# The last gate tile made wide, with the first down-projection products between its own and its results joined by folds

## The chip, the cores and the metric

The kernel runs on one core of a Trainium2 chip. The metric is the device time of one execution in microseconds (us). PE is the matrix engine, DVE the vector engine, ACT the scalar engine, POOL the general engine (here it mostly issues DMAs that add into their target), SP the engine that issues the loads from HBM.

## The reference

One decoder layer over 512 tokens with 1024 features: attention and retention, a layer norm, then a feed-forward part, in float32. The change touches only the feed-forward part:

```python
gate, up = jnp.split(x @ w_gate_up, 2, axis=-1)
ffn = (jax.nn.silu(gate) * up) @ w_down
return layer_norm(DEEPNORM_ALPHA * x + ffn, ln_ffn_gain, ln_ffn_bias)
```

The hidden width is 2816, in 22 tiles of 128 columns.

## The kernel before

**Splits.** A float32 product is made of three passes on PE over rounded parts: high by high, high by low, low by high. `split` (L85) makes the high part with an ACT copy (L86, a CAST) and the low part with a DVE subtraction (L91) or, for some operands, with an ACT negation and an adding DMA issued by POOL (L88, L89).

**Gate tiles.** The 22 tiles `n` are computed one after another. Each takes seven products of a Strassen-like scheme, into three PSUM banks `ga`, `gb` and `gc`; the weights of the products are called A, B, C and D, and the tokens' parts `11`, `12`, `22`, `s1` to `s4`. A *narrow* product (`g_mm`, L999) is twelve matmuls of 256 columns: for each of four slices of the contraction high by high, low by high, high by low. A *wide* product (`g_run`, L986) puts the two parts of the tokens side by side: four matmuls of 512 columns with the high weights and four of 256 with the low weights. The wide result has two halves that still have to be added. That is done by a *fold* (L939): ACT copies the bank into a temporary, DVE adds another bank where needed, and POOL issues a DMA of 128 KB that adds the right half to the left one. Tiles 4 to 20 are wide (`wide`, L935), the first four and the last, 21, are narrow. In a wide tile the results `w1`, `w2`, `t2` and `t7` are each folded; `w_silu1` and `w_silu2` apply SiLU on ACT to the folded `w1` and `w2`, and `w_end` (L1050, L1051) multiplies them by the folded `t2` and `t7` on DVE, into `hu`.

**Order.** The kernel is scheduled by hand: what each engine does, it does in the order in which the code names it. `w_cycle(n)` runs a wide tile, with products of the tile before and the tile after between its own. `g_cycle(21)` runs the last one, with `prepare_down` between its steps, and `g_end(21)` (L1033 to L1035) finishes it on DVE without a fold.

**Down projection.** The left half of the output is accumulated in four banks `left` (`dl0` to `dl3`, one for 128 tokens each). `conv_w(0, m)` splits the weights of a pair of hidden tiles `m` into `dh(0, m)` and `dl(0, m)`, `conv_h(m)` the hidden values into `h0` and `h1`; `d_mm` makes six matmuls of 512 columns for a bank. Pairs 0, 1, then 2, 3 and 10 are done so. Pair 10 is tiles 20 and 21, so it needs `w_end(20)` and the end of tile 21. Then come 21 units `w_mm(i)` of twelve matmuls each (a Strassen-like scheme for the rest), whose weights come from loads `r1`, `r2a`, `r2b`, `r3a` and so on. These loads use three buffers `raw`: `r2a` takes the buffer of `r1_2`, `r2b` that of `r1_3`, `r3a` that of `r1_4`, each when the last reader of the old contents is done. `r1_2` and `r1_3` are read by an ACT copy, an ACT negation and an adding DMA of POOL (L89, `dlp<-r`). The weights of a unit have four buffers, and `t4_` (L1425) and `t2_` (L1421) combine loads on DVE.

An ACT instruction on `idle` (L1525) stands behind the last SiLU, so that the function table of the square root is loaded there.

Of the kernel before, what the change touches and what calls it, by code (L numbers as in the profile page):

```python
# [53 lines left out]
def hybrid_layer_kernel(ctx: ExitStack, tc: tile.TileContext, xT, x, pos, w0, wf, wt, wo,  # L54
# [18 lines left out]
    def tmp(name, dt=F32):  # L73
        return tp.tile([P, 512], dt, tag="t", name=name)
# [856 lines left out]
    def held(n):  # L931
        return n in (0, 1)


    def wide(n):  # L935
        return FIRST <= n < NF - 1

    def fold(t):
        nc.gpsimd.dma_start(t[:, :Q], t[:, Q:], accum_op=ALU.add)  # L939
# [41 lines left out]
    def g_run(n, acc, kind, i, q, first, low, last):  # L981
        w = gw[n, kind][low]
        full = gp[n][acc]
        for k in range(4):
            rhs = parts[q][:, k, 0] if low else parts[q][:, k].rearrange("p i c -> p (i c)")
            T.matmul(full[:, :Q] if low else full, lhsT=w[:, i * S + k * P:i * S + k * P + P], rhs=rhs,  # L986
                     start=first and not low and k == 0, stop=last and k == 3, skip_group_check=True)

    def g_mm(n, acc, kind, i, q, first, low_first=False):
        h, l = gw[n, kind]  # L990
        if wide(n):
            for low in (1, 0) if low_first else (0, 1):
                g_run(n, acc, kind, i, q, first, low, low != low_first)
            return
        steps = [(k, a, b) for k in range(4) for a, b in ((h, 0), (l, 0), (h, 1))]
        if n == 0:
            steps.sort(key=lambda x: x[2])
        for j, (k, a, b) in enumerate(steps):
            T.matmul(gp[n][acc], lhsT=a[:, i * S + k * P:i * S + k * P + P], rhs=parts[q][:, k, b],  # L999
                     start=first and j == 0, stop=j == 11, skip_group_check=True)  # L1000
# [30 lines left out]
    def g_end(n):  # L1031
        g = gp[n]
        V.tensor_tensor(g["t2"], g["t2"], g["c"], op=ALU.add)  # L1033
        V.tensor_tensor(g["h1"], g["h1"], g["t2"], op=ALU.mult)
        V.tensor_tensor(g["h2"], g["h2"], g["t7"], op=ALU.mult)  # L1035

    def w_take2(n):
        g = gp[n]
        V.tensor_tensor(g["t2"], g["t2"], g["c"], op=ALU.add)  # L1039
        fold(g["t2"])  # L1040
# [4 lines left out]
    def w_silu2(n):  # L1045
        A.activation(gp[n]["h2"], gp[n]["w2"][:, :Q], AF.Silu)

    def w_end(n):
        g = gp[n]
        V.tensor_tensor(g["h1"], g["h1"], g["t2"][:, :Q], op=ALU.mult)  # L1050
        V.tensor_tensor(g["h2"], g["h2"], g["t7"][:, :Q], op=ALU.mult)  # L1051

    def w_copy2(n):
        g = gp[n]
        g["w2"] = tmp(f"w2_{n}")
        A.copy(g["w2"], g["a"])
        fold(g["w2"])

    def w_cycle(n):
        first, last = n == FIRST, n + 1 == NF - 1  # L1060
        p, nxt, g = n - 1, n + 1, gp[n]
        if first:
            g_mm(n, "a", "A", 0, "s2", False, True)
            g_end(p)
        else:
            g_run(p, "a", "C", 1, "22", False, 0, True)
            w_copy2(p)
            g_sum2(nxt)
            g_conv(n, "C")
            g_run(p, "c", "D", 0, "s4", False, 0, False)  # L1070
            g_run(n, "a", "A", 0, "s2", False, 0, False)
        g["c"] = psu(f"gc{n}")
        g_run(n, "c", "A", 1, "s1", True, 0, False)
        g_open(nxt)
        if not last:
            g_run(nxt, "a", "B", 0, "11", True, 0, False)
        if not first:
            g_run(n, "a", "A", 0, "s2", False, 1, True)
            g_run(p, "c", "D", 0, "s4", False, 1, True)
        g_run(n, "c", "A", 1, "s1", True, 1, True)  # L1080
        if last:
            g_mm(nxt, "a", "B", 0, "11", True)
        else:
            g_run(nxt, "a", "B", 0, "11", True, 1, True)
        if not first:
            if wide(n - 2):
                w_end(n - 2)
            g_conv(n, "D")
            g_load(n + 3)
            w_take2(p)  # L1090
        g["t2"] = tmp(f"t2_{n}")
        A.copy(g["t2"], g["a"])  # L1092
        g_conv(nxt, "A")
        g_mm(n, "a", "C", 0, "s3", False, True)
        g_t1(nxt)
        w_silu1(n)
        g["t7"] = tmp(f"t7_{n}")
        A.copy(g["t7"], g["a"])
        if last:
            g_mm(nxt, "b", "B", 1, "12", True)  # L1100
        else:
            for low in range(2):
                g_run(nxt, "b", "B", 1, "12", True, low, low == 1)
        g_sum3(nxt)
        V.tensor_tensor(g["t7"], g["t7"], g["c"], op=ALU.add)
        fold(g["t7"])
        g_run(n, "a", "C", 1, "22", False, 1, False)
        g_sum01(n + 2)
        g_u1(nxt)
        if wide(p):  # L1110
            w_silu2(p)
        g_conv(n + 2, "B")
        if last:
            g_run(n, "a", "C", 1, "22", False, 0, True)
            g_mm(n, "c", "D", 0, "s4", False)
            g_conv(nxt, "C")
            w_copy2(n)
            g_conv(nxt, "D")
            w_end(p)

    def g_cycle(n, between=None):
        nxt = n + 1 if FIRST <= n + 1 < NF else None
        g_mm(n, "a", "A", 0, "s2", False)
        if n and wide(n - 1):
            w_take2(n - 1)
        elif n and not held(n - 1):
            g_end(n - 1)
        if between:
            next(between)
        gp[n]["c"] = psu(f"gc{n}")[:, :Q]  # L1130
        g_mm(n, "c", "A", 1, "s1", True)
        t = tmp(f"gt{n}")
        gp[n]["t2"], gp[n]["t7"] = t[:, :Q], t[:, Q:]
        A.copy(gp[n]["t2"], gp[n]["a"])
        if n == 1:
            for m in range(FIRST):
                g_silu1(m)
        if n not in (1, 2, 3):
            g_conv(n + 1, "A")
        if nxt:  # L1140
            g_open(nxt)
            g_mm(nxt, "a", "B", 0, "11", True)
        g_mm(n, "a", "C", 0, "s3", False)
        if nxt:
            g_t1(nxt)
            g_mm(nxt, "b", "B", 1, "12", True)
        if held(n - 1):
            g_mm(n - 1, "c", "D", 0, "s4", False)
        if n == 0:
            g_mm(3, "b", "B", 1, "12", True)  # L1150
        c = gp[n]["c"]
        if n == NF - 1:
            c = tmp("gc")[:, :Q]
            A.copy(c, gp[n]["c"])
            g_mm(n, "c", "D", 0, "s4", False)
        A.copy(gp[n]["t7"], gp[n]["a"])
        if n == 0:
            for b in (2, 3):
                combine("s4", b)
                hi("s4", b)  # L1160
            g_sum(1, V, slice(2, 4))
        if n == 1:
            g_conv(2, "A")
            g_sum(2, V, slice(2, 4))
        V.tensor_tensor(gp[n]["t7"], gp[n]["t7"], c, op=ALU.add)
        if n in (2, 3):
            g_conv(n + 1, "A")
        if between:
            next(between)
        if n == 2:  # L1170
            g_end(n - 1)
        if n + 2 >= FIRST:
            g_conv(n + 2, "B")
        if n == 0:
            g_add1(3)
        g_mm(n, "a", "C", 1, "22", False)
        if nxt:
            g_u1(nxt)
        if n > 2:
            g_sum01(n + 2)  # L1180
            g_sum2(n + 2)
        g_conv(n + 1, "C")
        if n == 1:
            g_end(0)
        if n in (1, 2):
            g_sum(n + 2)
        if n == 0:
            for b in (2, 3):
                lo("s4", b)
            g_sum(2, V, slice(0, 2))  # L1190
        if n < NF - 1 and not held(n):
            g_mm(n, "c", "D", 0, "s4", False)
        if wide(n - 1):
            w_silu2(n - 1)
        A.activation(gp[n]["h2"], gp[n]["a"], AF.Silu)
        g_conv(n + 1, "D", V if n else None)
        g_load(n + 4)
# [300 lines left out]
        V.scalar_tensor_tensor(y[b][:, cs], in0=y[b][:, cs], scalar=r[:, 0:1], in1=gf[:, 1, cs], op0=ALU.mult, op1=ALU.add)  # L1498
        dma(out[b * P:(b + 1) * P, cs], y[b][:, cs])

    def prepare_down():
        conv_w(0, 0)
        conv_h(0)
        yield
        conv_w(0, 1)
        conv_h(1)
        yield

    for n in range(FIRST):
        g_cycle(n)  # L1510
# [2 lines left out]
    d_load(0, 0)  # L1513
    w_cycle(NF - 2)
    d_load(0, 1)
    g_cycle(NF - 1, prepare_down())
    g_end(NF - 1)

    def r1_load(j):
        r1[j] = raw_load(f"r1_{j}", [(2 * q, wd[2 * j + q, :, 0]) for q in range(2)])  # L1520
# [1 line left out]
    def r4_load(j):  # L1522
        r4[j] = raw_load(f"r4_{j}", [(2 * q, wd[2 * j + q, :, :, S:]) for q in range(2)])

    A.activation(idle, idle, AF.Sqrt)  # L1525
    left = [psu(f"dl{b}") for b in range(NB)]
    r1_load(2)
    d10 = [tmp(f"d10_{i}") for i in range(2)]
    for i in range(2):
# [1 line left out]
    r1_load(3)  # L1531
    conv_w(0, 2)
    conv_h(2)
    for b in range(3):
        for i in range(2):
            d_mm(left[b], 0, i, b, i == 0, False)
    conv_w(0, 3)
    r1_load(4)
    conv_h(3)
    for i in range(2):  # L1540
        d_mm(left[3], 0, i, 3, i == 0, False)
    for j in UNITS:
        s1_(j)
    for j in UNITS:
        aprep(1, j, blk(j, 0, 0), None)
    w_end(NF - 2)
    conv_h(10)
    t1_(2)
    conv_w(0, 10)
# [232 lines left out]
```

## Time and profile before

| | |
|---|---|
| median of 3 runs | 609.21 us (609.1 to 609.33) |
| the profiled execution | 609.27 us |
| its span, first to last instruction | 607.4 us |
| PE busy | 599.9 us (99%) |
| DVE busy | 517.3 us (85%) |
| ACT busy | 359.9 us (59%) |
| POOL busy | 187.8 us (31%) |
| stage of the last gate tile (its first to its last product) | 473.71 to 488.03 us |

A row of the timeline gives the start and the length of one or several merged instructions, engine, line, operation, target and sources, shape and count; a bracket names the idle time of the engine ahead of it and what ended it. `q1` is the queue of SP's loads, `q0` that of POOL's DMAs. A row of DMA issues gives count, size of each and the time from issue to landing.

### The profile page before, as it was taken

How to read it: one execution, taken by the hardware profiler on the slowest of the kernel's cores; microseconds unless marked ns; L12 is line 12 of the kernel's file. 1: busy time of each engine (PE TensorE's matmuls, PEld its weight loads, DVE VectorE, ACT ScalarE, POOL GpSimd, SP SyncE). 2: the span in 40 equal slices, each digit the busy share in tenths (PEclk: the TensorE clock that was granted, in tenths of full speed). 3: DMA queues.
4: the chain of work that ended last, by engine and by line, in shares of the span. 5: the costliest groups of instructions: out<-in, count | busy, mean ns of one | idle time of the engine just before them, and what ended most of it. 6: DMA issues, size and time to landing. Idle time of an engine off the chain costs nothing.

```text
span 607.4 us, 9356 instructions
## 1 busy us (share of the span) xinstructions
PE 599.9 (99%) x3280; PEld 522.2 (86%) x3280; DVE 517.3 (85%) x945; ACT 359.9 (59%) x633; POOL 187.8 (31%) x208
## 2 busy tenths in 40 slices
PE   8999999999999999999999999999999999999996
PEld 7988888888888888889998888888888988888885
DVE  6879976897997898989999898988889888988756
ACT  5454444434662766777657776776777685675300
POOL 0038732332363000342013444435344321241010
PEclk9999999999999999999999999999999999999999
DMA  8887864698984765596348888888887889699602
GB/s 280 251 249 195 219 208 123 151 225 225 204 174 108 278 227 202 126 249 129 87 154 202 165 208 164 209 188 186 205 173 191 183 224 204 158 249 228 249 35 105
DMA packets 50575, 115.25 MB, mean 190 GB/s; under 512 B 9136, under 2 KB 24816, under 8 KB 45024
## 3 DMA queue, kind: packets, MB, share of 16 engines
q1 hardware_dynamic: 25808, 77.68, 38.8%
q0 software_dynamic: 24416, 36.64, 34.8%
q8 instruction: 26, 0.43, 0.3%
q10 hardware_dynamic: 304, 0.33, 0.2%
q14 instruction: 21, 0.17, 0.1%
HBM read 74.52 MB, written 2.10 MB: 126 GB/s over the span
## 4 chain that ended last, share of the span: by engine, by line
PE 96%; DVE 2%; ACT 1%; DMA 1%; SPq 0%; issue 0%
PE ga L986 16%; PE gc L986 8%; PE pf L94 5%; PE pf L95 5%; PE pf L96 5%; PE ga L999 5%; PE gb L986 4%; PE pt L95 4%; PE pt L94 4%; PE pt L96 3%; PE acc L218 2%; PE dl L96 2%; PE dl L94 2%; PE dl L95 2%; PE gc L999 2%; PE mx L96 2%
## 5 line engine op out<-in xcount | busy, mean ns | idle before, releaser
L86 ACT CAST wh<-raw 128x1024 fp32r<-128x1024 f32 x44 | 46.0, 1048 | 30.6 <-issue 11.4
L939 POOL DMA_DIRECT2D t<-t x34 | 29.2, 858 | 75.2 <-DVE t L1039 43.7
L94 PE MATMUL pf<-xh,wh 128*128 128x512 f32 x128 | 50.0, 391 | 0.0
L95 PE MATMUL pf<-xl,wh 128*128 128x512 f32 x128 | 49.9, 390 | 0.0
L96 PE MATMUL pf<-xh,wl 128*128 128x512 f32 x128 | 49.9, 389 | 0.0
L91 DVE TENSOR_TENSOR wl<-raw,wh 128x1024 fp32r<-128x1024 f32 x26 | 33.1, 1281 | 12.0 <-ACT wh L86 12.0
L939 POOL DMA_DIRECT2D w<-w x34 | 29.5, 1002 | 41.9 <-DVE w L1025 39.7
L94 PE MATMUL pt<-wh,xh 128*128 128x512 f32 (+1 forms) x96 | 38.5, 402 | 0.0
L95 PE MATMUL pt<-wl,xh 128*128 128x512 f32 (+1 forms) x96 | 37.0, 386 | 0.0
L96 PE MATMUL pt<-wh,xl 128*128 128x512 f32 (+1 forms) x96 | 36.7, 382 | 0.0
L481 POOL TENSOR_TENSOR rs<-ve,half 128x1 f32<-128x1 f32 (+1 forms) x10 | 10.5, 1051 | 77.6 <-DVE ve L480 77.5
L89 POOL DMA_DIRECT2D wl<-raw x18 | 16.6, 922 | 45.2 <-ACT wl L88 44.3
L96 PEld LDWEIGHTS pf<-xh,wl 128*128 128x128 f32 x128 | 24.0, 188 | 5.2
L95 PEld LDWEIGHTS pf<-xl,wh 128*128 128x128 f32 x128 | 24.1, 188 | 4.6
L94 PEld LDWEIGHTS pf<-xh,wh 128*128 128x128 f32 x128 | 24.0, 188 | 4.6
L443 DVE MAX8 m<-score 128x8 f32<-128x256 f32 (+2 forms) x48 | 26.8, 557 | 1.0
L444 DVE MATCH_REPLACE8 score<-m,score 128x256 f32<-128x256 f32 (+2 forms) x48 | 26.0, 542 | 0.0
L954 POOL DMA_DIRECT2D graw<-graw x17 | 24.6, 1448 | 1.3 <-issue 0.9
L426 ACT ACTIVATE lg<-lg 128x256 f32<-128x256 f32 (+2 forms) x24 | 10.8, 474 | 22.7 <-PE lg L425 20.7
L1092 ACT COPY t<-ga 128x512 f32<-128x512 f32 x17 | 10.0, 588 | 22.9 <-PE ga L986 22.9
L89 POOL DMA_DIRECT2D slot<-hu x9 | 10.8, 1272 | 33.5 <-ACT slot L88 28.7
L96 PEld LDWEIGHTS pt<-wh,xl 128*128 128x128 f32 x96 | 18.0, 188 | 3.3
(1220 smaller groups left out, 2012.8 us busy)
## 6 DMA issues: line engine op xcount, KB each, us to landing
graw<-in_wgu_dram SPq DMA_DIRECT2D x22, 1024.0 KB, 5.1
wl<-raw POOLq DMA_DIRECT2D x18, 512.0 KB, 5.2
raw<-in_wo_dram SPq DMA_DIRECT2D x8, 1024.0 KB, 4.8
raw<-in_wf_dram SPq DMA_DIRECT2D x7, 1024.0 KB, 6.4
raw<-in_wt_dram SPq DMA_DIRECT2D x6, 1024.0 KB, 5.5
r<-in_wd_dram SPq DMA_DIRECT2D x12, 512.0 KB, 6.3
w<-w POOLq DMA_DIRECT2D x34, 128.0 KB, 2.8
graw<-graw POOLq DMA_DIRECT2D x17, 256.0 KB, 4.1
```

The source lines that it names most:

```text
L86: A.copy(hi, src)
L89: nc.gpsimd.dma_start(lo.bitcast(F32), src, accum_op=ALU.add)
L91: eng_lo.tensor_tensor(lo, src, hi.bitcast(F32), op=ALU.subtract)
L94: T.matmul(acc, lhsT=lh, rhs=rh, start=first, stop=False, **kw)
L95: T.matmul(acc, lhsT=lh, rhs=rl, start=False, stop=False, **kw)
L96: T.matmul(acc, lhsT=ll, rhs=rh, start=False, stop=last, **kw)
L443: V.max(m8, a)
L444: V.match_replace(out=a, in_to_replace=m8, in_values=a, imm_value=TAKEN)
L939: nc.gpsimd.dma_start(t[:, :Q], t[:, Q:], accum_op=ALU.add)
L954: nc.gpsimd.dma_start(u[:, :S], u[:, S:], accum_op=ALU.add)
L986: T.matmul(full[:, :Q] if low else full, lhsT=w[:, i * S + k * P:i * S + k * P + P], rhs=rhs, start=first and not low and k == 0, stop=las ...
L999: T.matmul(gp[n][acc], lhsT=a[:, i * S + k * P:i * S + k * P + P], rhs=parts[q][:, k, b], start=first and j == 0, stop=j == 11, skip_group ...
```

## The change

Tile 21 becomes wide. `w_cycle(20)` loses its special ending, `g_cycle` its branch for the last tile, and a new `w_last(21)` takes the place of `g_cycle(21)`, `prepare_down` and `g_end(21)`. It puts the products of tile 21 between the last ones of tile 20, and the first products of the down projection (pair 0, banks 0, 1 and 2) between the last ones of tile 21. The results `w1`, `w2`, `t2` and `t7` of tile 21 are folded. `w_silu2(21)`, ahead of the table load, stands behind the split of pair 2; `w_end(20)` and `w_end(21)` stand ahead of the split of pair 10.

```diff
     def wide(n):
-        return FIRST <= n < NF - 1
+        return n >= FIRST
...
     def w_cycle(n):
...
-        if last:
-            g_mm(nxt, "a", "B", 0, "11", True)
-        else:
-            g_run(nxt, "a", "B", 0, "11", True, 1, True)
+        g_run(nxt, "a", "B", 0, "11", True, 1, True)
...
-        if last:
-            g_run(n, "a", "C", 1, "22", False, 0, True)
-            g_mm(n, "c", "D", 0, "s4", False)
-            g_conv(nxt, "C")
-            w_copy2(n)
-            g_conv(nxt, "D")
-            w_end(p)
...
+    def left_mm(m, b):
+        d_mm(left[b], 0, m, b, m == 0, False)
+
+    def w_last(n):
+        p, g = n - 1, gp[n]
+        g_run(n, "a", "A", 0, "s2", False, 1, False)
+        g_run(p, "a", "C", 1, "22", False, 0, True)
+        w_copy2(p)
+        g_run(n, "a", "A", 0, "s2", False, 0, True)
+        g_conv(n, "C")
+        g_run(p, "c", "D", 0, "s4", False, 0, False)
+        g["c"] = psu(f"gc{n}")
+        g_run(n, "c", "A", 1, "s1", True, 0, False)
+        g_run(p, "c", "D", 0, "s4", False, 1, True)
+        g_run(n, "c", "A", 1, "s1", True, 1, True)
+        g["t2"] = tmp(f"t2_{n}")
+        A.copy(g["t2"], g["a"])
+        w_end(p - 1)
+        g_conv(n, "D")
+        w_take2(p)
+        g_mm(n, "a", "C", 0, "s3", False, True)
         conv_w(0, 1)
+        g["t7"] = tmp(f"t7_{n}")
+        A.copy(g["t7"], g["a"])
+        V.tensor_tensor(g["t7"], g["t7"], g["c"], op=ALU.add)
+        fold(g["t7"])
+        left_open()
+        left_mm(0, 0)
         conv_h(1)
-        yield
+        w_silu2(p)
+        w_silu1(n)
+        g_mm(n, "a", "C", 1, "22", False)
+        w_copy2(n)
+        left_open()
+        left_mm(0, 1)
+        g_mm(n, "c", "D", 0, "s4", False)
+        w_take2(n)
+        for b in (2, 3):
+            left_open()
+        left_mm(0, 2)
...
     d_load(0, 1)
-    g_cycle(NF - 1, prepare_down())
-    g_end(NF - 1)
+    conv_w(0, 0)
+    conv_h(0)
+    w_last(NF - 1)
...
-    A.activation(idle, idle, AF.Sqrt)
-    left = [psu(f"dl{b}") for b in range(NB)]
...
     conv_w(0, 2)
     conv_h(2)
+    w_silu2(NF - 1)
+    A.activation(idle, idle, AF.Sqrt)
     for b in range(3):
-        for i in range(2):
-            d_mm(left[b], 0, i, b, i == 0, False)
+        left_mm(1, b)
     conv_w(0, 3)
...
-    w_end(NF - 2)
+    for n in (NF - 2, NF - 1):
+        w_end(n)
     conv_h(10)
```

On PE, at the end of tile 20's products, before (`ga21` is bank `ga` of tile 21, `gh21A` the high part of its weights A):

```order
L986 MATMUL gc20_5006<-parts4_2890,gh20D_5039 128x512 x4
L986 MATMUL gc20_5006<-parts4_2890,gl20D_5040 128x256 x4
L999 MATMUL ga21_5011<-parts2_2692,gh21A_5047 128x256
L999 MATMUL ga21_5011<-parts2_2692,gl21A_5048 128x256
L999 MATMUL ga21_5011<-parts2_2692,gh21A_5047 128x256 x2
```

And now, from the last run of tile 20 to the first matmuls of the down projection:

```order
L986 MATMUL gc20_5006<-parts4_2890,gl20D_5036 128x256 x4
L986 MATMUL gc21_5116<-parts1_2756,gl21A_5044 128x256 x4
L986 MATMUL ga21_5011<-parts3_2695,gl21C_5107 128x256 x4
L986 MATMUL ga21_5011<-parts3_2695,gh21C_5106 128x512 x4
L94 MATMUL dl0_5155<-dh(0, 0)_5083,h0_0_5087 128x512
L95 MATMUL dl0_5155<-dl(0, 0)_5084,h0_0_5087 128x512
L96 MATMUL dl0_5155<-dh(0, 0)_5083,h1_0_5088 128x512
```

Tile 21's product with A now runs ahead of tile 20's end, and six matmuls of bank `dl0` stand between the two products with C, where the one with D stood.

On ACT, around the last SiLU (L1046 is `w_silu2`, into `hu5`; L1525 before and L1545 now is the instruction on `idle`, with its table load), before:

```order
L1046 ACTIVATE hu5_4900<-w2_20_5105 128x256
L1195 ACTIVATE hu5_4900<-ga21_5011 128x256
L1525 ACT_TABLE_LOAD
L1525 ACTIVATE idle_312<-idle_312 128x4
L86 CAST dh(0, 2)_5220<-draw0_1_5114 128x1024
L86 CAST h0_1_5224<-hu1_3175 128x1024
L86 CAST dh(0, 3)_5264<-draw0_1_5114 128x1024
```

And now (L1056 is the copy of the bank in `w_copy2`):

```order
L1056 COPY w2_21_5174<-ga21_5011 128x512
L86 CAST dh(0, 2)_5212<-draw0_1_5080 128x1024
L86 CAST h0_1_5216<-hu1_3175 128x1024
L1046 ACTIVATE hu5_4900<-w2_21_5174 128x256
L1545 ACT_TABLE_LOAD
L1545 ACTIVATE idle_312<-idle_312 128x4
L86 CAST dh(0, 3)_5240<-draw0_1_5080 128x1024
```

The last SiLU read a bank of PE; it now reads `w2_21`, which POOL's fold completes, and all that ACT does for the pairs 3 and 10 and for `r1` stands behind it.

On POOL, the end of the folds, before:

```order
L939 DMA w2_20_5105<-w2_20_5105 128x256
L939 DMA t2_20_5045<-t2_20_5045 128x256
L89 DMA slot0_5291<-hu2_3589 128x2x256
L89 DMA slot0_5291<-hu3_4026 128x2x256
L89 DMA slot1_5298<-hu4_4463 128x2x256
```

And now:

```order
L939 DMA w2_20_5099<-w2_20_5099 128x256
L939 DMA t2_20_5041<-t2_20_5041 128x256
L939 DMA t7_21_5151<-t7_21_5151 128x256
L939 DMA w2_21_5174<-w2_21_5174 128x256
L939 DMA t2_21_5129<-t2_21_5129 128x256
```

Three folds of tile 21 follow that of `t2_20`; the fourth, of `w1_21`, stands ahead of `w2_20`.

More of the change, by code (lines that the diff above doesn't have):

```diff
@@ L1059, in w_cycle @@
     def w_cycle(n):
-        first, last = n == FIRST, n + 1 == NF - 1
+        first = n == FIRST
         p, nxt, g = n - 1, n + 1, gp[n]
@@ L1074, in w_cycle @@
         g_open(nxt)
-        if not last:
-            g_run(nxt, "a", "B", 0, "11", True, 0, False)
+        g_run(nxt, "a", "B", 0, "11", True, 0, False)
         if not first:
@@ L1098, in w_cycle @@
         A.copy(g["t7"], g["a"])
-        if last:
[L1100 to L1103, printed above, removed]
+        g_mm(nxt, "b", "B", 1, "12", True)
         g_sum3(nxt)
@@ L1112, in w_cycle, with g_cycle @@
         g_conv(n + 2, "B")
-        if last:
-            g_run(n, "a", "C", 1, "22", False, 0, True)
-            g_mm(n, "c", "D", 0, "s4", False)
-            g_conv(nxt, "C")
-            w_copy2(n)
-            g_conv(nxt, "D")
-            w_end(p)
-    def g_cycle(n, between=None):
+    def g_cycle(n):
         nxt = n + 1 if FIRST <= n + 1 < NF else None
         g_mm(n, "a", "A", 0, "s2", False)
-        if n and wide(n - 1):
-            w_take2(n - 1)
-        elif n and not held(n - 1):
+        if n and not held(n - 1):
             g_end(n - 1)
-        if between:
-            next(between)
         gp[n]["c"] = psu(f"gc{n}")[:, :Q]
@@ L1151, in g_cycle @@
         c = gp[n]["c"]
[L1152 to L1155, printed above, removed]
         A.copy(gp[n]["t7"], gp[n]["a"])
@@ L1167, in g_cycle @@
             g_conv(n + 1, "A")
-        if between:
-            next(between)
         if n == 2:
@@ L1190, in g_cycle @@
             g_sum(2, V, slice(0, 2))
-        if n < NF - 1 and not held(n):
+        if not held(n):
             g_mm(n, "c", "D", 0, "s4", False)
-        if wide(n - 1):
-            w_silu2(n - 1)
         A.activation(gp[n]["h2"], gp[n]["a"], AF.Silu)
@@ L1499, in scale_bias, with left_open @@
         dma(out[b * P:(b + 1) * P, cs], y[b][:, cs])
-    def prepare_down():
-        conv_w(0, 0)
-        conv_h(0)
-        yield
-        conv_w(0, 1)
-        conv_h(1)
-        yield
+    left = []
+    def left_open():
+        left.append(psu(f"dl{len(left)}"))
+    def left_mm(m, b):
[18 more added lines that the diff above has]
+        g_mm(n, "a", "C", 0, "s3", False, True)
+        conv_w(0, 1)
+        g["t7"] = tmp(f"t7_{n}")
[4 more added lines that the diff above has]
+        left_mm(0, 0)
+        conv_h(1)
+        w_silu2(p)
[9 more added lines that the diff above has]
+        left_mm(0, 2)
     for n in range(FIRST):
@@ L1539, in hybrid_layer_kernel @@
     conv_h(3)
-    for i in range(2):
-        d_mm(left[3], 0, i, 3, i == 0, False)
+    for m in range(2):
+        left_mm(m, 3)
     for j in UNITS:
```

## The prediction

> **What bounds the kernel now.** I first read the waits of PE, from 460 us to the end. There is one, in the last microseconds:
>
> ```profile
> PE fin L1712 <- ACT diag L1711: 1.3, 1, 1.3
> ```
>
> From the last gate tiles on, matmuls follow each other without a gap, so only two things can move the end here: fewer or shorter matmuls, or a new wait of PE. The timeline of PE gives the pitch of both shapes, and the chain that ended last the period of a wide tile:
>
> ```profile
> 471.37 1.07 PE L986 MATMUL gc<-parts,gh20A 128*128 128x512 f32 x4
> 472.28 0.64 PE L986 MATMUL ga<-parts,gl20A 128*128 128x256 f32 x4
> 472.75 0.64 PE L986 MATMUL gc<-parts,gl19D 128*128 128x256 f32 x4
> ...
> 473.00 0.59 ACT L1092 COPY t<-ga 128x512 f32<-128x512 f32 x1 [0.59 <-PE ga L986]
> ...
> 473.71 0.28 PE L999 MATMUL ga<-part,gh21B 128*128 128x256 f32 x1
> ...
> 475.15 0.64 PE L986 MATMUL ga<-parts,gl20C 128*128 128x256 f32 x4
> ...
> 476.56 0.28 PE L999 MATMUL gb<-part,gh21B 128*128 128x256 f32 x1
> ...
> 477.98 0.64 PE L986 MATMUL ga<-part,gl20C 128*128 128x256 f32 x4
> ...
> 480.77 0.28 PE L999 MATMUL ga<-parts,gh21A 128*128 128x256 f32 x1
> ...
> 488.03 0.40 PE L94 MATMUL dl<-dh(0, 0)_5131,h 128*128 128x512 f32 x1
> 488.26 0.40 PE L95 MATMUL dl<-dl(0, 0)_5132,h 128*128 128x512 f32 x1
> ...
> 455.28 1.89 PE ga L986 x12
> 465.03 1.89 PE ga L986 x12
> ```
>
> **The gain.** The seven narrow products of tile 21 take 1.44 (473.71 to 475.15), 1.42 and 7.26 us (five, 480.77 to 488.03): 10.12. Seven wide ones take the period of a wide tile, 465.03 - 455.28 = 9.75. So PE gains **0.37 us**. The columns are the same, 3072 a product; only four short matmuls fewer are issued. The down projection's matmuls are the same ones in another order, at no price.
>
> **Inside the tile.** From 472.28 on I lay the runs in their new order: 0.91 us for four of 512, 0.48 for four of 256, 0.23 for a matmul of the down projection (488.03 to 488.26). ACT copies a bank in 0.59, from 0.08 behind the end of the run (473.00, after 472.28 + 0.64). Each accumulation into `ga21` that follows a copy of the bank must wait for ACT. The tightest place is the copy for `t7_21`: the run ahead of it ends at 485.0, the copy at 485.7, and the six matmuls of `dl0` (1.36 us) hold PE until 486.2. They hide it by 0.5; without them it would cost about 0.7. The others have as much or more, so I put this part at 0, and at 0.7 for its worse end.
>
> **The new wait.** The last product with C ends near 487.8 in the new order. ACT copies `w2_21` until 488.45; POOL answers such a copy 0.29 us later (481.17 after 480.30 + 0.58), so the fold is issued at 488.75. Now `w_silu2(21)` waits for its landing, and behind it on ACT stand the table load, pair 3, six operations on `slot`, pair 10, and the copies of `r1`. Before, that SiLU read PSUM, 0.30 us behind PE.
>
> ```profile
> 480.30 0.58 ACT L1056 COPY w<-ga 128x512 f32<-128x512 f32 x1
> 481.17 0.86 POOL L939 DMA_DIRECT2D w<-w  x1 [1.95 <-ACT w L1056]
> 488.23 0.38 ACT L1195 ACTIVATE hu<-ga 128x256 f32<-128x256 f32 x1 [0.30 <-PE ga L999]
> 490.04 1.03 ACT L86 CAST dh(0, 2)_5220<-draw 128x1024 fp32r<-128x1024 f32 x1
> ```
>
> How long does a fold take? The profile's page says 2.8 us for those of `w` and 4.7 for those of `t`, and single windows show why they differ:
>
> ```profile
> w<-w POOLq DMA_DIRECT2D x34, 128.0 KB, 2.8
> t<-t POOLq DMA_DIRECT2D x34, 128.0 KB, 4.7
> ...
> 483.68 0.86 POOL L939 DMA_DIRECT2D t<-t  x1 [1.66 <-DVE t L1039]
> ...
> q1 hardware_dynamic: 268, 0.95, 97.4%
> t<-t POOLq DMA_DIRECT2D x1, 128.0 KB, 8.0
> ...
> q1 hardware_dynamic: 281, 0.52, 74.8%
> q0 software_dynamic: 129, 0.12, 38.5%
> ```
>
> The two `q1` rows are of 484 to 488 and of 488 to 490 us. The fold issued at 483.68 moved nothing for four microseconds, in which the loads filled the engines; its 0.12 MB went through after 488, and it landed after 8.0 us. So a fold waits for the loads issued ahead of it. Those loads are these:
>
> ```profile
> 481.43 0.69 DVE L91 TENSOR_TENSOR gl21D<-graw,gh21D 128x512 fp32r<-128x512 f32 x1 [0.23 <-ACT gh21D L86]
> 482.15 0.83 SPq L80 DMA_DIRECT2D r<-in_wd_dram  x2
> 483.08 0.96 SPq L80 DMA_DIRECT2D d<-in_wd_dram  x2
> 486.70 1.23 DVE L91 TENSOR_TENSOR dl(0, 1)_5183<-draw,dh(0, 1)_5182 128x1024 fp32r<-128x1024 f32 x1 [0.52 <-ACT dh(0, 1)_5182 L86]
> 487.96 7.47 SPq L80 DMA_DIRECT2D r<-in_wd_dram  x4
> ```
>
> `r1_2` was issued as `gl21D` freed its buffer, `r1_3` as `dl(0, 1)` did. In the new order `gl21D` must wait for its buffer until the low half of tile 20's D has run, at 483.15, and ends at 483.94: `r1_2` goes at 484.0, with `d10` behind it. `dl(0, 1)` moves ahead, to 485.7, so `r1_3` goes at 485.9. That is 2.6 MB back to back, all issued before the fold of `w2_21`, with two other folds ahead of it on its queue. I take the nearest row, 8.0 us: **landing at 496.75**. At the 0.95 MB that 484 to 488 moved, the loads alone need 11 us from 485.5, to 496.5; with three folds of 0.77 us (38.5% of two) behind them, the upper end is 10 us, 498.8. The lower end is 2.8 us, 491.55.
>
> The Trainium skill ("DMA: Bandwidth & Descriptors", section "Queues, rings and completion order") says that each DMA engine takes turns between the queues for which it has work, packet by packet. By that a fold would not wait for the loads, and the sum would be that of rival A below, 608.9 to 610.8. In the windows above it did wait, so I go by them.
>
> **What follows from it.** ACT's next weights came 1.81 us behind the last SiLU (488.23 to 490.04). So `dh(0, 3)` starts at 498.7 and the high part of pair 3 ends at 500.7; DVE takes 1.14 for its low part, 1.8 for three sums, 1.36 for four halves of `w_end`, and the split of pair 10 starts at 505.2 where it was at 498.30: **6.9 us late**. From there on ACT's order is dense except for 0.77 us ahead of the second `dhp<-r`, so that copy is 6.1 late.
>
> ```profile
> 498.30 1.05 ACT L86 CAST h<-hu 128x1024 fp32r<-128x1024 f32 x1 [1.24 <-DVE hu L1051]
> 504.62 1.05 ACT L86 CAST dhp<-r 128x1024 fp32r<-128x1024 f32 x1 [0.77 <-ACT slot L86]
> ...
> 506.93 1.19 POOL L89 DMA_DIRECT2D dlp<-r  x1 [3.14 <-DVE tw L1411]
> 513.55 2.88 SPq L80 DMA_DIRECT2D r2b<-in_wd_dram  x4
> 516.53 1.79 SPq L80 DMA_DIRECT2D r3a<-in_wd_dram  x4
> ...
> 523.14 2.68 DVE L1425 TENSOR_TENSOR tw<-r3a,r2a 128x512 f32<-128x512 f32 x4 [0.26 <-DMA r3a<-in_wd_dram]
> ...
> 529.34 2.35 DVE L91 TENSOR_TENSOR dlp<-r2a,dhp 128x1024 fp32r<-128x1024 f32 x2
> ...
> 531.80 0.39 PE L95 MATMUL dx<-dlp,slot 128*128 128x512 f32 x1
> ```
>
> The chain to PE: the adding DMA of 506.93 follows that copy; `r2b` waits for its landing (513.55), as it takes the buffer of `r1_3`; `r3a` stands behind `r2b` on SP; DVE already waits for `r3a` now (0.26 at 523.14), and behind that DVE is dense until the low weights of unit 6, the first of the two in the row at 529.34 (ready at 530.56, half of 2.35 later). PE reads them at 531.80. So the slack is 1.24 us, and 0.37 less when PE comes earlier: 0.87. With the chain 6.1 late, PE stalls **5.2 us** there. (Unit 1, five times twelve matmuls earlier, reads what the adding DMA makes; 513.4 + 6.1 is 1.7 us after its 517.8, a part of the same 5.2.) Behind unit 6, PE needs new weights every 2.7 us and DVE makes them in 1.2; I expect no more.
>
> **Sum.** 609.27 (this execution; the median of the three is 0.06 lower) - 0.37 + 5.2 = **614.1 us**. In general: a landing of L us puts the chain L - 1.9 late and stalls PE by L - 2.8. Its ends are 608.9 (L = 2.8, no stall) and 616.1 (L = 10).
>
> **Rivals.**
>
> *A. The fold does not queue behind the loads.* Then it lands after 2.8 us, or up to the 4.7 of the `t` row when it shares the engines with them. At 2.8, the stall is 0 and the time 608.9; at 4.7 it is 1.9, and 610.8. The point from which it decides is L = 3.2, where stall and gain cancel. For it: the folds of `w` took 2.8, 34 of them. Against: none of these was issued behind a load, and the next row shows what one does (window 495 to 499, in which three folds of `slot` were issued, the first at 495.26, behind the loads of `r1_4`):
>
> ```profile
> q1 hardware_dynamic: 132, 0.51, 75.7%
> slot<-hu POOLq DMA_DIRECT2D x3, 256.0 KB, 7.7
> ```
>
> No byte of these moved while the loads ran. Its likeliest time is 609.3, not slower than before. The rule of the Trainium skill that stands above ("DMA: Bandwidth & Descriptors") is this rival's.
>
> *B. The wait is there, but the slack is larger:* `r3a` lands as early as before, because with other loads shifted the queue is emptier. Then the stall is unit 1's alone, 1.7, and the time 610.6; with the adding DMA quicker by its queueing it would be 609 to 610. Against: `r3a` cannot be issued before `r2b`, nor that before the adding DMA has read its buffer.
>
> *C. The loads hold the fold longer* (L of 10 to 12): 616.1 to 618.1.
>
> *D. PE waits inside the tile as well,* by the 0.7 above once or twice: that is hidden in the sum if the later stall comes, as that is set by ACT's chain, and alone it gives 609.6 to 610.3.
>
> **How the numbers follow.** Main case (L of 5.5 to 10, 611.6 to 616.1): 0.58. A: 0.20, B and D with little stall: 0.15, C: 0.05; a shortening of PE's work by over 1.2 us that I do not see: 0.02. What differs by less than 0.2% (1.2 us, 608.0 to 610.4) can't be told from no change. All of A up to L = 4.3 and two thirds of B and D lie there: 0.28. Faster: 0.02. Slower: 0.70. The range runs from A's lower end, 608.8, to 616.3, which leaves out C and little else.
>
> **What would show it.** In the changed kernel's trace: wide products of tile 21 without a gap (the matmuls from the first with `gh21B` to the last of tile 21 and the eighteen of the down projection between them); `r1_3` issued near 486; the fold of `w2_21` landing near 497 and ACT's `hu<-w` waiting for a DMA for some 6 us ahead of the table load; `h<-hu` of pair 10 near 505; `r3a` near 522.5; PE waiting for DVE's `dlp` at unit 6, with a first wait at unit 1. A landing before 492 and no wait of PE would prove rival A. A wait of PE between 472 and 490 would prove D.

## The result, and the profile after

| | before | after |
|---|---|---|
| median | 609.27 us (6 runs, 608.92 to 609.56) | 612.66 us (6 runs, 612.22 to 613.13) |
| ratio | | 1.0052, 95% interval 1.0042 to 1.0063 |
| span of the profiled execution | 607.4 us | 610.9 us |

The changed kernel is 3.4 us slower; 614.1 was forecast. The waits of PE from 460 us on, where there was one before:

```profile
PE fin L1724 <- ACT diag L1723: 1.3, 1, 1.3
PE dx L95 <- DVE dlp L91: 1.1, 1, 1.1
PE dx L95 <- DMA dlp<-r: 1.1, 1, 1.1
PE dy L95 <- DVE dlp L91: 0.3, 1, 0.3
```

No wait lies inside the tile; the three new ones are at units 1 (`dx`, for an adding DMA), 5 (`dy`) and 6 (`dx`, for low weights of DVE). The profiled executions aren't aligned in this stage: the run with `gh20A`, which the change doesn't touch, starts at 471.69 and not 471.37, so **0.32 us** is to be taken off a time of after before it is compared. The timeline of PE, with that run, the first matmul of pair 2, and the places where the pitch (the time from one start to the next, 0.227 us here) breaks:

```profile
471.69 1.07 PE L986 MATMUL gc<-parts,gh20A 128*128 128x512 f32 x4
...
498.88 0.39 PE L94 MATMUL dl<-dh(0, 2)_5212,h 128*128 128x512 f32 x1
...
509.76 0.39 PE L94 MATMUL dl<-dh(0, 10)_5289,h 128*128 128x512 f32 x1
510.10 0.50 PE L95 MATMUL dl<-dl(0, 10)_5290,h 128*128 128x512 f32 x1
510.44 0.39 PE L96 MATMUL dl<-dh(0, 10)_5289,h 128*128 128x512 f32 x1
...
518.18 0.39 PE L94 MATMUL dx<-dhp,slot 128*128 128x512 f32 x1
519.64 0.50 PE L95 MATMUL dx<-dlp,slot 128*128 128x512 f32 x1 [1.07 <-DMA dlp<-r]
519.98 0.39 PE L96 MATMUL dx<-dhp,slot 128*128 128x512 f32 x1
...
531.10 0.50 PE L95 MATMUL dy<-dlp,slot 128*128 128x512 f32 x1 [0.29 <-DVE dlp L91]
...
535.24 0.50 PE L95 MATMUL dx<-dlp,slot 128*128 128x512 f32 x1 [1.12 <-DVE dlp L91]
```

*The gain is there.* From the run with `gh20A` to pair 2, PE needs 498.88 - 471.69 = 27.19 us; before, the same stretch took 498.94 - 471.37 = 27.57. That is 0.38 less, where 0.37 was forecast.

*The loss.* A place loses what two starts are apart beyond 0.227, in the pitch at the wait and the one behind it: 0.23 at pair 10, 1.35 at unit 1, 0.56 at unit 5, 1.40 at unit 6, in all **3.5 us**. With the gain, 3.5 - 0.4 = 3.1. From the run with `gh20A` to the first matmul of `fin`, near the end, PE needs 132.15 us where it needed 128.86, 3.3 more and near the 3.4 between the medians; the missing tenth or two is in the next pitches behind each wait, of 0.23 to 0.24 us.

The chain behind it, in the timelines of ACT, DVE, POOL and SP:

```profile
488.13 0.59 ACT L1056 COPY w<-ga 128x512 f32<-128x512 f32 x1 [0.59 <-PE ga L986]
489.01 0.86 POOL L939 DMA_DIRECT2D w<-w  x1 [1.16 <-ACT w L1056]
497.50 0.42 ACT L1046 ACTIVATE hu<-w 128x256 f32<-128x256 f32 x1 [6.88 <-DMA w<-w]
499.33 1.03 ACT L86 CAST dh(0, 3)_5240<-draw 128x1024 fp32r<-128x1024 f32 x1
505.93 1.05 ACT L86 CAST h<-hu 128x1024 fp32r<-128x1024 f32 x1 [1.48 <-DVE hu L1051]
507.02 1.23 DVE L91 TENSOR_TENSOR h<-hu,h 128x1024 fp32r<-128x1024 f32 x1 [1.12 <-ACT h L86]
511.39 1.05 ACT L86 CAST dhp<-r 128x1024 fp32r<-128x1024 f32 x1
513.70 1.19 POOL L89 DMA_DIRECT2D dlp<-r  x1 [2.27 <-DVE slot L91]
519.72 1.75 SPq L80 DMA_DIRECT2D r2b<-in_wd_dram  x4
521.57 2.54 SPq L80 DMA_DIRECT2D r3a<-in_wd_dram  x4
527.96 2.49 DVE L1398 TENSOR_TENSOR tw<-r3a,r2a 128x512 f32<-128x512 f32 x4
533.97 2.35 DVE L91 TENSOR_TENSOR dlp<-r2a,dhp 128x1024 fp32r<-128x1024 f32 x2
...
w<-w POOLq DMA_DIRECT2D x1, 128.0 KB, 8.4
```

The bracket at 497.50 is the new wait: ACT stands for 6.88 us for the fold of `w2_21` (last row: 8.4 us from issue to landing). The row to note is that of 527.96: it has **no bracket**. DVE doesn't wait for `r3a`; from 507.02 to 533.97 it has no pause at all.

### The profile page after: what moved, and what is told of

Read it like the earlier page. It is cut to its first block, busy times and chain, and to the rows that moved or that the text cites. A ratio compares the mean times of both kernels' runs of the same rounds, so it can differ in the third digit from the quotient of the medians.

```text
span 610.9 us, 9316 instructions
## 1 busy us (share of the span) xinstructions
PE 601.8 (99%) x3252; PEld 521.3 (85%) x3252; DVE 518.0 (85%) x945; ACT 360.3 (59%) x633; POOL 191.1 (31%) x212
## 4 chain that ended last, share of the span: by engine, by line
PE 64%; issue 15%; POOL 11%; DVE 6%; DMA 2%; ACT 1%; POOLq 0%; DVEq 0%; ACTq 0%
PE pf L94 5%; PE pf L95 5%; PE pf L96 5%; POOL t L939 4%; PE ga L999 4%; POOL graw L954 4%; PE pt L95 4%; PE pt L94 4%; PE pt L96 3%; PE acc L218 3%; POOL w L939 3%; PE mx L94 2%; PE mx L96 2%; PE mx L95 2%; PE gc L999 2%
## 5 line engine op out<-in xcount | busy, mean ns | idle before, releaser
L939 POOL DMA_DIRECT2D t<-t x36 | 30.8, 857 | 79.7 <-DVE t L1039 48.1
L939 POOL DMA_DIRECT2D w<-w x36 | 31.4, 1000 | 42.0 <-DVE w L1025 39.9
L94 PEld LDWEIGHTS pt<-wh,xh 128*128 128x128 f32 x96 | 18.1, 188 | 2.8
```

The source lines that it names most:

```text
L94: T.matmul(acc, lhsT=lh, rhs=rh, start=first, stop=False, **kw)
```

## The experiments

All kernels are made from the changed one. Each was run beside the kernel before on one chip; the ratio is to that. The chips differ between the runs, so their ratios and traces are compared rather than their medians.

### 1. Where the wait harms: ACT's order, the fold

`e1_silu_later` moves the SiLU and the table load behind the operations on `slot`:

```diff
-    w_silu2(NF - 1)
-    A.activation(idle, idle, AF.Sqrt)
     for b in range(3):
...
+    w_silu2(NF - 1)
+    A.activation(idle, idle, AF.Sqrt)
     for n in (NF - 2, NF - 1):
         w_end(n)
```

> Everything of the change stays; only the last SiLU (w_silu2 of tile 21) and the table load behind it move on ACT, from ahead of pair 3 to behind the six operations on slot, just ahead of the last w_end. The fold still lands near 497.4, but ACT has done pair 3 and slot by then. Theory (ACT's queue, held by the wait for the fold, is what costs): the copy of pair 10 starts near 499.4 and not 505.9, PE has no wait between 490 and 600, and the time is 608.9 (before less the 0.37 us of the shorter products). Rival (the loss is from other parts: the order on PE, the two more half-products on DVE, the loads that moved): it stays near 612.7.

`e2_no_fold` leaves the fold of `w2_21` out, so that its right half is missing from the SiLU's input:

```diff
-        w_copy2(n)
+        g["w2"] = tmp(f"w2_{n}")
+        A.copy(g["w2"], g["a"])
```

> The fold of w2_21 is left out, so the last SiLU reads only the left half of the sum (the second half of tile 21's hidden values is without its low-weight part). All else stands in place. Theory: ACT does not wait, SiLU runs near 490.6, no stall of PE, 608.9. Rival (loss from elsewhere): 612.7.

Measured: 608.81 us, ratio 0.9992 (0.9984 to 1.0001), and 608.57, ratio 0.9989 (0.998 to 0.9998). In both, PE's only wait from 460 us on is the one at the end, as before. In the first the fold still lands after 8.4 us; ACT's timeline shows it splitting pair 3 meanwhile:

```profile
490.74 1.05 ACT L86 CAST dh(0, 3)_5238<-draw 128x1024 fp32r<-128x1024 f32 x1
...
497.75 0.42 ACT L1046 ACTIVATE hu<-w 128x256 f32<-128x256 f32 x1 [1.88 <-DMA w<-w]
```

So the whole loss comes from ACT standing for this fold with its queue behind it. A late fold alone costs nothing.

### 2. How long the fold waits, and for what

A load of 2 KB that reads `w2_21` is put on SP's queue; what stands behind it there isn't issued before the fold has landed. In `e3_r13_behind_fold` it stands ahead of `r1_3`, in `e4_all_behind_fold` ahead of `r1_2`, in `e8_one_load_ahead` ahead of `d10`:

```diff
+    mark = sp.tile([P, 4], F32, tag="nsum", name="mark")
+    dma(mark, gp[NF - 1]["w2"][:, :4])
     r1_load(3)
```

> A load of 2 KB from w2_21 stands on SP's queue ahead of the load of r1_3, so r1_3 is issued only when the fold has landed; r1_2 and d10 (1.5 MB) still go ahead of it. Theory (the fold waits for the loads issued ahead of it): landing after 4 to 5.5 us instead of 8.4, so ACT is held some 3.5 us less, and of the 3.5 us of stalls nothing or up to 0.5 is left: 608.9 to 609.5. Rival (the fold is slow by itself, by its place behind two other folds on POOL's queue): landing stays above 7 us and the time near 612.7.

> The same load of 2 KB stands ahead of r1_2, so none of the 2.6 MB is issued before the fold has landed. Theory: landing after 2.8 to 3.2 us, as for the folds of w elsewhere, SiLU near 492. The loads come some 7 us later than in the changed kernel; r1_2 and d10 are needed near 501, r1_3 near 504.5, so they may cost up to 1 us: 608.9 to 610. Rival (fold slow by itself): landing above 6 us, 612 to 613.

> The changed kernel in which d10 and r1_3 wait for the fold of w2_21 and only r1_2 (1 MB) is issued ahead of it. Known: 3.1 us with none ahead, 6.2 with r1_2 and d10 (1.5 MB), 8.4 with all (2.6 MB). If a fold waits for the bytes issued ahead of it, it lands after 3.5 to 5 us and nothing stalls (608.7 to 609.0). If it shares the engines by turns, the landing is 2.8 to 3.5. If the number of loads and not their bytes sets it, about 5 to 6, and PE stalls up to 1 us (609.5).

The landing is from the rows of DMA issues, the split of pair 10 is counted from the start of ACT's copy of `w2_21`, and PE's loss is in pitch as above:

| kernel | issued ahead of the fold | landing, us | split of pair 10, us | PE's loss, us | median, us | ratio |
|---|---|---|---|---|---|---|
| `e4` | none | 3.1 | 12.48 | 0 | 608.74 | 0.9994 (0.9984 to 1.0003) |
| `e8` | 1.0 MB | 4.8 | 14.24 | 0 | 609.15 | 1.0004 (0.9995 to 1.0013) |
| `e3` | 1.6 MB | 6.2 | 15.61 | 1.4 | 609.94 | 1.0009 (1.0 to 1.0019) |
| after | 2.6 MB | 8.4 | 17.80 | 3.5 | 612.66 | 1.0052 (1.0042 to 1.0063) |

The rows of `e3` in the timelines of ACT, DVE and PE (those of after stand above):

```profile
503.89 1.05 ACT L86 CAST h<-hu 128x1024 fp32r<-128x1024 f32 x1 [1.49 <-DVE hu L1051]
504.98 1.23 DVE L91 TENSOR_TENSOR h<-hu,h 128x1024 fp32r<-128x1024 f32 x1 [1.12 <-ACT h L86]
...
531.94 2.35 DVE L91 TENSOR_TENSOR dlp<-r2a,dhp 128x1024 fp32r<-128x1024 f32 x2
...
533.20 0.50 PE L95 MATMUL dx<-dlp,slot 128*128 128x512 f32 x1 [1.12 <-DVE dlp L91]
```

The landing grows with what is issued ahead, with the same three folds in line on POOL's queue. Bytes and the number of loads (0, 2, 4 and 6) grow together here; `e8`'s 4.8 us lies in the range forecast for bytes and just under that for the number, which doesn't settle it. The loss is the landing less **4.9 us**, and zero below it (8.4 and 3.5; 6.2 and 1.4; 4.8 and 0). The prediction had the landing less 2.8: the slope is right and the slack 2.1 us too small.

Where that slack lies, `e3` shows beside after: from DVE's part of the split of pair 10 to the low weights of unit 6 it is 531.94 - 504.98 = 26.96 us here and 533.97 - 507.02 = 26.95 there, both without a pause. What came late was DVE's own work, not `r3a`.

### 3. DVE's work or `r3a`

In `e5_sums_later` the three sums `s3_` (1.89 us of DVE at 519.53 in the profile after) are moved behind unit 6's weights, in `e9_sums_spread` the same three steps earlier:

```diff
-    for j in UNITS:
-        s3_(j)
...
         elif 8 <= i <= 10:
+            s3_(UNITS[i - 8])
             aprep(7, UNITS[i - 8], pq(t3s[UNITS[i - 8]]), None)
```

```diff
         if 5 <= i <= 7:
             aprep(4, UNITS[i - 5], blk(UNITS[i - 5], 1, 1), None)
+            s3_(UNITS[i - 5])
```

> The changed kernel with the three sums s3_ (1.8 us of DVE) moved from ahead of pair 10's split to a place after unit 6. Theory 1 (the stall at units 5 and 6 is DVE's own work: without a pause from the split of pair 10, 507.02, to the low weights of unit 6, 533.97; the same 26.95 us, 504.98 to 531.94, stand in the kernel whose last load waited for the fold): all of it starts 1.2 to 1.8 us earlier, the waits at units 5 and 6 shrink by as much, and the time falls to 610.9 to 611.5. Theory 2 (the prediction's: unit 6 is set by the adding DMA, r2b and r3a in a row): the second dhp<-r copy follows ACT's order; if ACT's pair 10 copy does not move, r3a and unit 6 do not, and the time stays at 612.7. ACT's copy of pair 10 waits for DVE's w_end halves (1.5 us before it), so theory 2 too can give up to 1.5 us, if that copy moves by as much; DVE's pauses between 507 and 534 then tell the two apart: none under theory 1.

> The changed kernel with the three sums s3_ again moved behind unit 6's weights, but one each behind the weights of units 8, 9 and 10, a step ahead of where ACT reads them (in the run before, they stood at that step itself, and a wait of 1.9 us and a half-speed clock followed at 563 us). If that late loss came from their place: PE waits at unit 1 (about 1.0 us) and unit 6 (about 1.0) and nowhere behind; the loss falls from 3.5 us of pitch to 2.8, as r3a is next in line 0.7 us behind DVE's work, and the time from 612.7 to 612.0. If DVE's work alone set units 5 and 6 it would be 611. If the late loss does not depend on their place, 614 to 615 again.

> The changed kernel itself, beside the run with the spread sums on the same chip: 612.7, with 3.5 us of lost pitch at pair 10 and units 1, 5 and 6.

(The first expectation puts the sums ahead of pair 10's split; in the trace they stood behind it, at 519.53. It is DVE's work between the split and unit 6 all the same.)

Measured: 614.89 us, ratio 1.009 (1.0075 to 1.0105); 612.32, ratio 1.0042 (1.0025 to 1.0059); and the change itself again 612.38, ratio 1.0049 (1.0034 to 1.0064). DVE and PE in `e9`:

```profile
526.76 2.67 DVE L1398 TENSOR_TENSOR tw<-r3a,r2a 128x512 f32<-128x512 f32 x4 [0.77 <-DMA r3a<-in_wd_dram]
532.96 2.35 DVE L91 TENSOR_TENSOR dlp<-r2a,dhp 128x1024 fp32r<-128x1024 f32 x2
...
534.23 0.50 PE L95 MATMUL dx<-dlp,slot 128*128 128x512 f32 x1 [0.91 <-DVE dlp L91]
...
562.00 0.50 PE L95 MATMUL dx<-dlp,slot 128*128 128x512 f32 x1 [0.28 <-DVE dlp L91]
```

Without the sums DVE at once waits for `r3a` (0.77; 0.83 in `e5`), and unit 6's weights come only 0.77 us earlier behind the split of pair 10 (532.96 - 505.69 = 27.27 where it was 533.97 - 505.93 = 28.04). So both limits are there: DVE's work is the later one, and `r3a` stands **0.8 us** behind it. Theory 1 was right on what set the end and wrong on the price, as taking 1.8 us out exposes the next wait after 0.8. In `e9` the wait at unit 5 is gone and that at unit 6 shorter, but a new one of 0.28 at 562.00 takes most of it back; the time can't be told from that of the change.

`e5` was a miss of mine: 2 us slower instead of 1.5 faster. The sums stood at the very step in which ACT reads them, and with ACT's copies behind them DVE paused 1.73 us three times; a later unit then came late by 1.88. Its PE timeline:

```profile
561.05 0.39 PE L94 MATMUL dx<-dhp,slot 128*128 128x512 f32 x1
563.33 0.50 PE L95 MATMUL dx<-dlp,slot 128*128 128x512 f32 x1 [1.88 <-DVE dlp L91]
563.66 0.52 PE L96 MATMUL dx<-dhp,slot 128*128 128x512 f32 x1
563.97 0.63 PE L94 MATMUL dx<-dhp,slot 128*128 128x512 f32 x1
564.40 0.63 PE L95 MATMUL dx<-dlp,slot 128*128 128x512 f32 x1
```

Behind that wait the pitch is 0.43 us instead of 0.227 until 566.96. `e9` shows that this came from the place of the sums: there the wait is 0.28 us, and the pitch is the usual one soon after.

### 4. The cover inside the tile

`e6_no_cover` is `e4` with the six `dl0` matmuls moved behind the second product with C, so that nothing stands between the copy of the bank for `t7_21` and the next accumulation into it:

```diff
-        left_open()
-        left_mm(0, 0)
         conv_h(1)
         w_silu2(p)
         w_silu1(n)
         g_mm(n, "a", "C", 1, "22", False)
         w_copy2(n)
+        left_open()
+        left_mm(0, 0)
         left_open()
         left_mm(0, 1)
```

> The kernel in which all three loads wait for the fold (608.7), with the six products of the down projection that stand between tile 21's two C products moved behind the second one. If they hide the copy t7_21, as the prediction has it, PE now waits some 0.7 us for that copy ahead of the second C product, and the time is 0.7 us higher, 609.4. Rival: PE's own time hides it anyway or the wait is taken up later: no change, 608.7.

Measured: 609.63 us, ratio 1.0006 (0.9997 to 1.0014). PE's timeline:

```profile
485.19 1.20 PE L986 MATMUL ga<-part,gh21C 128*128 128x512 f32 x4 [0.67 <-ACT t L1502]
```

The wait is as forecast. From the run with `gh20A` to pair 2 PE needs 28.17 us instead of 27.20, so it costs 0.97 rather than 0.7; the restart costs some tenths beside the wait. A second wait, of 0.23 us, follows at unit 6 (532.28): DVE had stood 1.89 us for `r3a` before it could make those weights, where it stood 1.10 in `e4`. Up to `fin`, `e6` so needs 1.49 us more than `e4` in the traces; by the intervals of their ratios alone the two can't be told apart.

### 5. Both repairs together

> The changed kernel with both repairs: the loads wait for the fold, and ACT's second SiLU and table load stand behind the slot operations. If the wide products gain 0.37 us of PE and nothing waits any more, 608.9, 0.06% under the kernel before. If the repairs hold independent gains, 608.3. If the table load hurts at its new place, 609.3 or more.

`e7_both` has the edits of `e1` and `e4`. Measured: 609.01 us, ratio 0.9998 (0.9986 to 1.001). The repairs are not independent: each takes the wait away wholly. From the run with `gh20A` to pair 2, `e1`, `e2`, `e4`, `e7` and `e8` all need 27.19 or 27.20 us, so the gain of 0.38 stands in each trace, and up to `fin` it is 128.48 to 128.54 us where it was 128.86. Their five ratios lie between 0.9989 and 1.0004, and only the interval of `e2`, which leaves the fold out, stays below 1. A version with the wide tile is thus about as fast as the kernel before, perhaps 0.05% faster; that it beats it isn't shown.

## Why the prediction was right, and where its size was off

- **The gain of 0.37 us**: right, 0.38 in the trace of after and in five other kernels.
- **Inside the tile, nothing**: right. No wait of PE between the products, and without the six matmuls the copy holds PE for 0.67, where 0.7 was forecast.
- **The fold behind the loads**: right in place and nearly in size. The fold was issued at 489.01 and took 8.4 us, not 8.0. That the two are so near is partly luck: in the row that gave 8.0 the 1.6 MB of loads began 1.5 us ahead of the fold, here 2.6 MB began 4.7 us ahead, and with 1.6 MB and those 4.7 us it took 6.2 (`e3`). Rival A is out: with 2.6, 1.6, 1.0 and 0 MB issued ahead, the landing takes 8.4, 6.2, 4.8 and 3.1 us. The picture of a queue behind all the loads was too simple, though. The shares of the queues in after, in 485 to 490, 490 to 491 and 491 to 492 us, and the issues of `r1_3`:

```profile
q1 hardware_dynamic: 276, 1.03, 83.9%
...
q1 hardware_dynamic: 150, 0.29, 79.5%
q0 software_dynamic: 44, 0.05, 27.8%
...
q1 hardware_dynamic: 106, 0.19, 58.9%
q0 software_dynamic: 96, 0.09, 56.7%
...
r<-in_wd_dram SPq DMA_DIRECT2D x2, 512.0 KB, 10.7
```

  From 485 to 490 the folds' queue has no row, though two folds of `t` were issued by then; from then on both queues move side by side. It is the fold of `t2_20`, the first in line, that waits: in after, `e3` and `e8` the folds' bytes begin to move between 489.5 and 490.75, with 0.9 to 1.3 MB of loads through, whether 1.0, 1.6 or 2.6 MB are queued by then. That is about the 1.0 MB of `r1_2`, which alone was issued ahead of that fold in all three (`d10` follows it by 0.05 us in after). Most of what `d10` and `r1_3` add to the landing, they add later, while both queues move. What the loads lose by it isn't shown: `r1_3` takes 10.7 us (last row) and 5.1 in `e3`, where it was issued behind the fold, but here 1.6 MB of loads stood ahead of it as well. The rule of the Trainium skill ("DMA: Bandwidth & Descriptors", section "Queues, rings and completion order"), turns between the queues packet by packet, agrees with the second stretch and not with the first. No run here shows what holds the folds back in the first; with the same work on POOL and DVE and no load ahead (`e4`), the two folds of `t` land after 2.6 us, where it was 8.6.
- **ACT's order**: right. Pair 3's weights at 499.33 - 0.32 = 499.01 (forecast 498.7), the split of pair 10 at 505.61 (505.2), the second `dhp<-r` at 511.07 (510.7), `r2b` at 519.40 (519.65): each within about 0.4 us.
- **The chain `r2b`, `r3a`, unit 6: here the size was off.** The prediction carried the whole delay through it as the trace of before had it. There, from the issue of `r2b` to the use of `r3a` by DVE it was 523.14 - 513.55 = 9.6 us. Without the cover of DVE's work it is 7.3 to 7.4 us now (`e9`: 519.46 to 526.76; `e5`: 518.87 to 526.24). It has no fixed price, though: in `e4` and `e6`, where DVE waits for `r3a` too, it is 8.6 and 10.1. In after, SP spends 1.75 instead of 2.88 us on `r2b`, and `r3a` lands 5.4 us after its issue instead of 6.9. The rows of DMA issues, first of before, then of after:

```profile
r2b<-in_wd_dram SPq DMA_DIRECT2D x4, 256.0 KB, 3.9
r3a<-in_wd_dram SPq DMA_DIRECT2D x4, 256.0 KB, 6.9
```

```profile
r2b<-in_wd_dram SPq DMA_DIRECT2D x4, 256.0 KB, 5.0
r3a<-in_wd_dram SPq DMA_DIRECT2D x4, 256.0 KB, 5.4
```

  So `r3a` would have let unit 6 start 0.8 us earlier than it did, and DVE's work set it. DVE could make up time because it had paused before, for 0.86, 1.43 and 0.26 us in the stretch from 505 to 529; these 2.55 us are gone in after. Unit 6's weights came 533.97 - 0.32 - 529.34 = 4.3 us late instead of 6.1; less the slack of 0.87 that is 3.4 us of loss, as measured. The forecast of 5.2 was high by 1.7: 2.1 of slack that it didn't have, less the 0.4 that the fold came later than forecast. This is the part of rival B that came true: `r3a` was quicker, though not as early as before.
- **Unit 1** lost 1.35 of the total, where 1.7 was forecast. Unit 5 lost 0.56 and pair 10 0.23, which the prediction had not listed.

What is open: why the issue of `r2b` took 2.88 us before and 1.75 in every run of the changed kernel, and why `r3a` lands after anything from 4.8 us (`e10`) to 8.5 (`e6`).

## What to carry to other kernels

When a result that was read straight from PSUM now comes through a DMA, look at what the engine that waits for it has queued behind, and put that first: here the same late fold cost 3.5 us ahead of the queue and nothing behind it. A late DMA is best priced from loads already issued when it is, and here the landing grew with what was issued ahead of it. A delay does not travel through a chain at full size: add up the pauses of every engine along it, and look for the second limit that takes over when the first is moved.

## What was unexpected in the hardware

A wait of PE of 1.88 us in `e5` was followed by more than 3 us at half the clock. The stretches, with the columns time, sum, busy times of PE, its weight loads, DVE, ACT and POOL, the granted clock, the DMA share and GB/s:

```profile
563.00:563.70 0.70, 0.37 (x2) 0.33 (x3) 0.70 (x2) 0.00 (x0) 0.00 (x0) 1.00 1.05 319
563.70:565.00 1.30, 1.30 (x5) 1.00 (x4) 0.78 (x2) 1.05 (x1) 0.00 (x0) 0.53 1.13 307
565.00:567.00 2.00, 2.00 (x7) 1.52 (x6) 2.00 (x3) 1.04 (x1) 0.00 (x0) 0.50 1.04 262
```

The clock falls only after PE has started again, at 563.7, and the slow matmuls cost 1.7 us beside the wait. The waits of 1.1 us in after had no such consequence: the granted clock is 1.00 behind both. The Trainium skill ("TensorE: Matmul & The Clock Gate", section "Why this matters for your kernels") warns of gaps of more than about 3 us; here one of 1.88 was followed by half the clock, in the one trace that has such a gap behind 460 us, and no run here shows where the limit lies.
